# Two neighbouring blocks of convolution sums in one PSUM bank, and the gate stage buffers in pools of their own beside the dense part's first loads

## The chip, the cores and the metric

One core of a Trainium2 chip. The metric is the device time of one execution in microseconds. The kernel before took 3110.72 us, the median of three runs (3105.67 to 3121.32). The engines are TensorE (PE in the profile; its weight loads are PEld), VectorE (DVE), ScalarE (ACT), GpSimd (POOL) and SyncE (SP); matrix products accumulate in PSUM, eight banks of 128 x 512 float32.

## The reference

One decoder layer over 1024 tokens of 1024 channels. What matters here:

```python
z = rmsnorm(h) @ w_in                      # q, k, v, a, gt
attn = dilated_attention(rope(q), rope(k), v)
glu = a * sigmoid(gt)                      # 512 channels
c = causal_depthwise_conv(glu, conv_w) + conv_b     # 31 taps
h += concat(rmsnorm(attn), rmsnorm(silu(layernorm(c)))) @ w_out

# PEER: 8 heads x 16 experts of 16384 for each token
i1, i2, gate = product_key_top16(rmsnorm(h) @ w_q, sub_keys)
act = gelu(x . expert_u[i1 * 128 + i2]) * gate
h += sum(act * expert_v[i1 * 128 + i2])

h += sigmoid(rmsnorm(h) @ w_g) * (p @ w_p)
out = rmsnorm(h)
```

## The kernel before

Tokens lie in 8 tiles of 128, in four groups of two. Each group goes through the **front**: input projection (`qkv`, in `token_major`), attention, convolution (`convolve`), output projection (`mixed`, `project`), the search for experts (`search`, `combine`). The order of the stages is written out at L876 to L888; the projections of the next group start while the group before is still in its convolution and output stage.

PEER is then done in two ways. Tiles 0, 1, 6, 7 (`FEW`) are **gathered**: POOL fetches one row of `expert_u`, later of `expert_v`, per token by an indirect DMA (`fetch`, L609), VectorE multiplies it (L622) or adds it into `gy` (L638); 1024 such rows of 128 tokens in all, which fill VectorE and POOL beside everything else. Tiles 2 to 5 (`ALL`) are done in a **dense** way: a gate for each of the 16384 experts and 512 tokens is built by `gate_matrix` and written to DRAM (`gate_d`), and `dense` runs over all experts in 128 chunks of 128.

*The convolution.* `lin` is a set of three PSUM banks that nearly every projection uses: `q`, `k`, `v`, `a`, `gt`, `o`, `pq`, `pc`, the comparisons `pd`. In `convolve` the 512 channels are four blocks `c` of 128 channels by 256 tokens. For each, 13 taps are done beside (ScalarE scales a `tap`, POOL adds it into `side`, two buffers, L359 to L363), and 18 taps on VectorE, in place in a bank of `lin`, `cs` (L364 to L369). L371 adds the two into `cc`. A `cs` fills 256 of the 512 columns of its bank. The accumulators of `token_major` take one whole bank for each of the two token tiles.

*The seam.* `gate_matrix` fills, for each tile `j` and block `b` of 32 tokens, a `stage` of 128 x 128 x 32 values (two buffers of 16 KB a partition, pool `gp`) and stores it to `gate_d` with one DMA of 2 MB on SyncE's queue (L700). When the 16 stores are issued, `gp` is closed and `dupool` (`du`) is opened at the same place, the right-hand end of SBUF. `du` holds, for `dense`, the chunks of `uT` and their rounded and rest parts (`u`, `uh`, `ul`, two buffers of 4 KB each), `gt` (three buffers of 4 KB) and `gelu` (two of 2 KB).

*The dense part.* `columns(c)` loads chunk `c` of `uT` on SyncE's queue (L728), ScalarE rounds it (`uh`, L730), VectorE takes the rest (`ul`, L732). 24 matmuls (L754 to L756) sum into `ph`, which has two banks. ScalarE's `gelu` (L758) reads it, VectorE multiplies by the gates `gt` (L762), which are read back from `gate_d` (L741). After four chunks, 96 matmuls (L785 to L787) add the products with `expert_v` into `py`.

The order of instructions on each engine and queue is made by the framework's scheduler ahead of time, from its own costs and from the order in the source; it also places the tiles and sets the waits between engines. Memory of a pool that is closed is given to the next pool, whose tiles then wait for the last users of what they lie over.

Of the kernel before, what the change touches and what calls it, by code (L numbers as in the profile page):

```python
# [10 lines left out]
F32 = mybir.dt.float32  # L11
# [9 lines left out]
P = 128  # L21
# [12 lines left out]
DN = ND * P  # L34
# [11 lines left out]
NK = 128  # L46
# [5 lines left out]
GROUP = 4  # L52
BT = 32
# [48 lines left out]
def tile_layer(ctx, tc, t, consts, out):  # L102
    nc = tc.nc
# [6 lines left out]
    uT_d = t["uT"]  # L110
# [10 lines left out]
    def scope(parent, **kw):  # L121
        s = parent.enter_context(ExitStack())
        return s, s.enter_context(tc.tile_pool(bufs=1, **kw))
# [13 lines left out]
    lin, tps, sps, pps = bank(ps, "lin", 3), bank(ps, "tp", 1), bank(ps, "s", 2), bank(ps, "pt", 1)  # L137
# [199 lines left out]
    def convolve(g, xT):  # L337

        gn = xT.shape[2]
        glus = []  # L340
        for c in range(NCT):
            pg = channel_major(xT, w_ag, NCT + c, f"gt{g}_{c}")
            sg = mpool.tile([P, GN], F32, tag="t2", name=f"sg{g}_{c}", bufs=3)[:, :gn]
            S.activation(sg, pg, AF.Sigmoid)
            pa = channel_major(xT, w_ag, c, f"a{g}_{c}")
            glu = apool.tile([P, TAPS - 1 + GN], F32, tag="glu", name=f"glu{g}_{c}", bufs=NCT - 1)[:, : TAPS - 1 + gn]
            V.tensor_copy(glu[:, 0 : TAPS - 1], last[:, c, :])
            V.tensor_tensor(glu[:, TAPS - 1 :], pa, sg, ALU.mult)
            if g + 1 < NG:
                V.tensor_copy(last[:, c, :], glu[:, gn:])  # L350
            glus.append(glu)
        cT = []
        for c, glu in enumerate(glus):
            tap = lambda k: (glu[:, k : k + gn], cw[:, c, k : k + 1])
            side = apool.tile([P, GN], F32, tag="side", name=f"side{g}_{c}", bufs=2)[:, :gn]
            for k in range(SIDE_TAPS):
                xk, wk = tap(k)
                if k == 0:
                    S.activation(side, xk, AF.Copy, scale=wk)  # L359
                else:  # L360
                    m = apool.tile([P, GN], F32, tag="tap", name=f"tap{g}_{c}_{k}", bufs=3)[:, :gn]
                    S.activation(m, xk, AF.Copy, scale=wk)  # L362
                    G.tensor_tensor(side, side, m, ALU.add)  # L363
            sums = lin(f"cs{g}_{c}")[:, :gn]  # L364
            xk, wk = tap(SIDE_TAPS)
            V.tensor_scalar(sums, xk, wk, cw[:, c, TAPS : TAPS + 1], ALU.mult, ALU.add)
            for k in range(SIDE_TAPS + 1, TAPS):
                xk, wk = tap(k)
                V.scalar_tensor_tensor(sums, xk, wk, sums, ALU.mult, ALU.add)  # L369
            cc = apool.tile([P, GN], F32, tag="cc", name=f"cc{g}_{c}", bufs=4)[:, :gn]  # L370
            V.tensor_tensor(cc, sums, side, ALU.add)  # L371
            cT.append(cc)
        return cT
# [273 lines left out]
            gather_v(i, ex, act, y)  # L647
            yield i, y

    def gate_matrix(gp, j, i1, i2, gate):  # L650

        tr = []
        for what, src in (("i2", i2), ("g", gate)):
            f = flat(src)
            if what != "g":
                f32 = mpool.tile([P, SLOTS], F32, tag="t2", name=f"gl{what}{j}", bufs=3)
                S.copy(f32, f)
                f = f32
            pt = pps(f"pgt{what}{j}")
            nc.tensor.transpose(pt[:, 0:P], f, ident)  # L660
            d = gp.tile([P, P], F32, tag=f"{what}T", name=f"{what}T{j}", bufs=2)
            S.copy(d, pt[:, 0:P])
            tr.append(d)
        i2T, gT = tr
        i2N = gp.tile([P, P], F32, tag="i2N", name=f"i2N{j}", bufs=2)
        S.activation(i2N, i2T, AF.Copy, scale=-1.0)
        four = [P, 4, NK]

        def less_keys(ix, t0, name):

            pd = lin(name).rearrange("p (t k) -> p t k", k=NK)
            nc.tensor.matmul(pd, flat(ix), ident16[:, t0 : t0 + 4].unsqueeze(2).to_broadcast(four), start=True, stop=False)
            nc.tensor.matmul(pd, ones16, minus16.to_broadcast([1, 4, NK]), start=False, stop=True)
            return pd

        for b in range(P // BT):
            stage = gp.tile([P, NK, BT], F32, tag="stage", name=f"stage{j}_{b}", bufs=2)
            for o in range(0, BT, 4):
                t0 = b * BT + o
                oa = gp.tile(four, F32, tag="oa", name=f"oa{j}_{t0}", bufs=2)  # L680
                V.scalar_tensor_tensor(
                    oa, less_keys(i1, t0, f"pd1_{j}_{t0}"), 0.0, gT[:, t0 : t0 + 4].unsqueeze(2).to_broadcast(four),
                    ALU.is_equal, ALU.mult,
                )
                o2 = gp.tile(four, F32, tag="o2", name=f"o2_{j}_{t0}", bufs=3)
                if o % 8 == 0:
                    V.tensor_tensor(
                        o2, i2T[:, t0 : t0 + 4].unsqueeze(2).to_broadcast(four),
                        iota.unsqueeze(1).to_broadcast(four), ALU.is_equal,
                    )  # L690
                else:

                    for e in range(4):
                        S.activation(o2[:, e, :], iota, AF.Abs, bias=i2N[:, t0 + e : t0 + e + 1])
                    S.activation(o2, o2, AF.Relu, bias=1.0, scale=-1.0)
                pg = sps(f"pG{j}_{t0}")
                for e in range(4):
                    nc.tensor.matmul(pg[:, rows(e)], o2[:, e, :], oa[:, e, :], start=True, stop=True)  # L698
                S.copy(stage[:, :, o : o + 4], pg.rearrange("p (t i) -> p i t", i=NK))
            nc.sync.dma_start(gd[j, :, :, b], stage.rearrange("p (q c) t -> p q (c t)", c=GROUP))  # L700
# [13 lines left out]
                S.copy(hi, pt)  # L714
                V.tensor_tensor(lo, pt, hi.bitcast(F32), ALU.subtract)

    def dense(du, dp, dus, dps, h1, xh, xl, read):

        phs, pys = bank(dus, "ph", 2), bank(dps, "py", 2)

# [4 lines left out]
        def columns(c):  # L725

            u = du.tile([P, D], F32, tag="u", name=f"u{c}", bufs=2)
            nc.sync.dma_start(u, uT_d[c])  # L728
            hi = du.tile([P, D], F32R, tag="uh", name=f"uh{c}", bufs=2)
            S.copy(hi, u)  # L730
            lo = du.tile([P, D], F32R, tag="ul", name=f"ul{c}", bufs=2)
            V.tensor_tensor(lo, u, hi.bitcast(F32), ALU.subtract)  # L732
            return hi, lo

        ready = columns(0)
        for c0 in range(0, NK, GROUP):
            gts = []
            nb = DN // BT // 2
            for f in range(2):
                gt = du.tile([P, nb, GROUP, BT], F32, tag="gt", name=f"gt{c0}_{f}", bufs=3)  # L740
                nc.sync.dma_start(  # L741
                    gt.rearrange("p (j b) c t -> p j (b c t)", j=ND // 2),
                    gd[f * ND // 2 : (f + 1) * ND // 2, :, c0 // GROUP].rearrange("j p b c -> p j (b c)"),
                )
                gts.append(gt)
            ah, al, vh, vl = [], [], [], []
            for c in range(c0, c0 + GROUP):
# [4 lines left out]
                for k in range(KD):  # L752
# [1 line left out]
                    nc.tensor.matmul(ph, hi, xh[:, k, :], start=k == 0, stop=False)  # L754
                    nc.tensor.matmul(ph, hi, xl[:, k, :], start=False, stop=False)  # L755
                    nc.tensor.matmul(ph, lo, xh[:, k, :], start=False, stop=k == KD - 1)  # L756
                ge = du.tile([P, DN], F32, tag="gelu", name=f"gelu{c}", bufs=2)
                S.activation(ge, ph, AF.Gelu)  # L758
                ge3 = ge.rearrange("p (b t) -> p b t", t=BT)
                for f in range(2):  # L760
                    g = ge3[:, f * nb : (f + 1) * nb]
# [3 lines left out]
                b = dp.tile([P, DN], F32R, tag="al", name=f"al{c}", bufs=GROUP)  # L765
# [7 lines left out]
                b = dp.tile([P, D], F32R, tag="vl", name=f"vl{c}", bufs=GROUP)  # L773
# [67 lines left out]
    fetched, wide, h1s = {}, {}, {}  # L841
# [47 lines left out]
    xh = hilo.tile([P, KD, DN], F32R, name="xh")  # L889
    xl = hilo.tile([P, KD, DN], F32R, name="xl")  # L890
    gph, gp = scope(ctx, name="gph", side="right")
    h1 = dict(zip(sum(GROUPS, ()), sum((h1s[g] for g in range(NG)), [])))
    h1 = [h1[i] for i in ALL]
    ident16 = gp.tile([P, P], BF16, name="ident16")
# [4 lines left out]
    V.tensor_scalar(minus16[:, 0, :], iota[0:1, :], -1.0, None, ALU.mult)  # L899
    stage_search(NG - 1)  # L900
    for j, i in enumerate(ALL):
        gate_matrix(gp, j, *wide[i])
    stage_combine(NG - 1)
    wide_input(h1, xh, xl)
    gph.close()
    den_in, du = scope(ctx, name="dupool", side="right")
    mix.close()
    mix_ps.close()
    ep = ctx.enter_context(tc.tile_pool(name="epool", bufs=1))
# [7 lines left out]
    def read():  # L917

        den_in_ps.close()
        den_in.close()  # L920
        split.close()
        tail = ctx.enter_context(tc.tile_pool(name="tail", bufs=1, side="right"))
        tail_ps = ctx.enter_context(tc.tile_pool(name="tail_ps", bufs=1, space=PSUM, side="right"))
        for f in range(2):
            for k in range(KD // 2 + 1):
                kept[k, f] = embed_weight(tail, f"wt{k}{f}", k, f)
        tails.extend((tail, bank(tail_ps, "pg", 2)))

    dense(du, dp, dus, dps, h1, xh, xl, read)
    den_ps.close()  # L930
    den.close()
    late_ps = ctx.enter_context(tc.tile_pool(name="late_ps", bufs=1, space=PSUM))
# [64 lines left out]
```

## Time and profile before

| | |
|---|---|
| median of three runs | 3110.72 us (3105.67 to 3121.32) |
| the profiled execution | 3121.36 us, its span 3119.6 us |
| TensorE busy | 2736.8 us (88%) |
| VectorE busy | 2505.5 us (80%) |
| POOL busy | 1504.7 us (48%) |
| ScalarE busy | 1129.3 us (36%) |
| mean granted clock of TensorE | 0.948 |
| moved by DMA | 868.89 MB, mean 279 GB/s |

Busy time says what an engine does, and not what the end waits for. For that there are the chain of waits (the work that ended last, followed back step by step), the list of who waited for whom, and the timeline of one engine, where the time an engine sat idle ahead of an instruction stands in brackets with what ended it. A line of a timeline can stand for several instructions of one form (x12); its duration is then that of the whole run. "L369" is a line of the kernel.

### The profile page before, as it was taken

Reading aid. Unit: us, or ns where it says so; the run is one execution under the profiler, and the core shown is the slowest. Engines: PE = TensorE matmul, PEld = TensorE weight load, DVE = VectorE, ACT = ScalarE, POOL = GpSimd, SP = SyncE. Lnnn points to the kernel's source line nnn. Section 1 sums busy time; section 2 is a strip of 40 time slices with the busy share of each in tenths; the row PEclk is TensorE's granted clock in tenths of the full one; section 3 lists DMA queues with packets and bytes.
Section 4 is the critical chain, followed back from the end, with each engine's and each line's share of the span. In section 5 each row is a group of like instructions: output and inputs, shape, how many; then the busy total and the mean of one; then the engine's idle time right before and its main releaser. Section 6 shows DMA issues by size and latency. Waiting matters only on the chain.

```text
span 3119.6 us, 36029 instructions
## 1 busy us (share of the span) xinstructions
PE 2736.8 (88%) x11711; PEld 2003.7 (64%) x11711; DVE 2505.5 (80%) x5164; ACT 1129.3 (36%) x2083; POOL 1504.7 (48%) x1220
## 2 busy tenths in 40 slices
PE   5689969978995789959999999999999999999986
PEld 2456635753773476647777777877777777777543
DVE  1527877988898799968888888988888888888882
ACT  3532534363245249942322222222223223222342
POOL 0300876464445420135665565665565555655670
PEclk9889978989997899989999999999999999999998
DMA  5244869747853866899999999999998999998991
GB/s 193 68 162 129 300 232 353 268 136 278 314 184 121 309 209 179 241 324 330 349 351 326 321 340 333 366 348 337 345 327 321 343 342 338 347 335 299 348 336 58
DMA packets 305390, 868.89 MB, mean 279 GB/s; under 512 B 26874, under 2 KB 93842, under 8 KB 305202
## 3 DMA queue, kind: packets, MB, share of 16 engines
q0 software_dynamic: 147456, 536.94, 47.4%
q1 hardware_dynamic: 154480, 326.30, 30.3%
q10 hardware_dynamic: 3266, 3.36, 0.3%
q8 instruction: 92, 1.51, 0.2%
q14 instruction: 96, 0.79, 0.1%
HBM read 822.98 MB, written 43.52 MB: 278 GB/s over the span
## 4 chain that ended last, share of the span: by engine, by line
PE 32%; DVE 20%; issue 17%; DMA 14%; POOL 11%; ACT 5%; POOLq 0%; ACTq 0%; DVEq 0%; SPq 0%
POOL v L609 5%; DMA v<-in_expert_v_dram 5%; PE pG L698 4%; DVE gy L638 3%; POOL u L609 3%; POOL side L363 3%; DVE u L622 3%; DMA v<-in_expert_v_dram,ex 3%; DMA u<-in_expert_u_dram,ex 2%; PE plg L819 2%; PE pq L270 2%; PE s L389 2%; PE py L785 2%; DVE cs L369 2%; PE py L787 1%
## 5 line engine op out<-in xcount | busy, mean ns | idle before, releaser
L609 POOL DMA_INDIRECT u<-in_expert_u_dram,ex x512 | 675.5, 1319 | 794.4 <-DVE hk L622 508.8
L609 POOL DMA_INDIRECT v<-in_expert_v_dram,ex x512 | 673.6, 1316 | 533.9 <-DVE gy L638 366.3
L638 DVE SCALAR_TENSOR_TENSOR gy<-v,ga,gy 128x1024 f32<-128x1024 f32 x512 | 657.4, 1284 | 41.2 <-DMA v<-in_expert_v_dram,ex 31.7
L622 DVE CUSTOM_DVE_ANT_0 u<-u,gxn 128x1024 f32<-128x1024 f32 x512 | 616.6, 1231 | 46.3 <-DMA u<-in_expert_u_dram,ex 45.1
L754 PE MATMUL ph<-xh,uh 128*128 128x512 f32 x1024 | 405.5, 396 | 47.6 <-ACT uh L730 44.5
L756 PE MATMUL ph<-xh,ul 128*128 128x512 f32 x1024 | 406.9, 397 | 24.8 <-DVE ul L732 24.4
L772 ACT CAST vh<-v 128x1024 fp32r<-128x1024 f32 x128 | 131.5, 1051 | 770.0 <-PE kept_y L787 502.9
L755 PE MATMUL ph<-xl,uh 128*128 128x512 f32 x1024 | 402.4, 393 | 0.0
L363 POOL TENSOR_TENSOR side<-side,tap 128x256 f32<-128x256 f32 x192 | 155.4, 810 | 214.0 <-ACT tap L362 147.5
L754 PEld LDWEIGHTS ph<-xh,uh 128*128 128x128 f32 x1024 | 194.5, 190 | 94.9 <-ACT uh L730 51.8
L756 PEld LDWEIGHTS ph<-xh,ul 128*128 128x128 f32 x1024 | 194.4, 190 | 80.5 <-DVE ul L732 40.1
L774 DVE TENSOR_TENSOR vl<-v,vh 128x1024 fp32r<-128x1024 f32 x128 | 154.2, 1223 | 112.4 <-ACT vh L772 112.2
L785 PE MATMUL py<-vh,ah 128*128 128x512 f32 x512 | 204.0, 398 | 42.3 <-ACT ah L764 42.3
L270 PE MATMUL pq<-x2T,w_pq 128*128 128x256 f32 x1024 | 230.3, 383 | 2.1 <-DMA w_pq<-in_peer_wq_dram 1.5
L755 PEld LDWEIGHTS ph<-xl,uh 128*128 128x128 f32 x1024 | 194.6, 190 | 40.9
L270 PEld LDWEIGHTS pq<-x2T,w_pq 128*128 128x128 f32 x1024 | 194.2, 192 | 30.1 <-issue 2.7
L785 PE MATMUL kept_y<-vh,ah 128*128 128x512 f32 x512 | 201.1, 393 | 0.0
L787 PE MATMUL kept_y<-vh,al 128*128 128x512 f32 x512 | 201.0, 393 | 0.0
L786 PE MATMUL kept_y<-vl,ah 128*128 128x512 f32 x512 | 201.0, 393 | 0.0
L786 PE MATMUL py<-vl,ah 128*128 128x512 f32 x512 | 199.8, 393 | 0.0
L787 PE MATMUL py<-vh,al 128*128 128x512 f32 x512 | 198.4, 395 | 0.3 <-DVE al L766 0.3
L730 ACT CAST uh<-u 128x1024 fp32r<-128x1024 f32 x128 | 134.1, 1048 | 106.6 <-DMA u<-in_uT_dram 74.9
(266 smaller groups left out, 4693.0 us busy)
## 6 DMA issues: line engine op xcount, KB each, us to landing
u<-in_uT_dram SPq DMA_DIRECT2D x128, 512.0 KB, 6.9
v<-in_expert_v_dram SPq DMA_DIRECT2D x128, 512.0 KB, 6.9
w_pq<-in_peer_wq_dram SPq DMA_DIRECT2D x64, 512.0 KB, 5.9
gate_d<-stage SPq DMA_DIRECT2D x16, 2048.0 KB, 10.7
gt<-gate_d SPq DMA_DIRECT2D x64, 512.0 KB, 10.7
w_o<-in_w_out_dram SPq DMA_DIRECT2D x32, 512.0 KB, 4.9
w_k<-in_w_qkv_dram SPq DMA_DIRECT2D x16, 512.0 KB, 4.6
w_q<-in_w_qkv_dram SPq DMA_DIRECT2D x16, 512.0 KB, 3.5
```

What stands on the lines that cost most here:

```text
L270: nc.tensor.matmul(a, w[:, k, :], xT[:, k, :], start=k == 0, stop=k == KD - 1)
L363: G.tensor_tensor(side, side, m, ALU.add)
L609: d = G.indirect_dma_start(out=e, out_offset=None, in_=table, in_offset=bass.IndirectOffsetOnAxis(ap=index, axis=0))
L622: uses(V.tensor_tensor_reduce(out=e, in0=e, in1=xn, scale=1.0, scalar=0.0, op0=ALU.mult, op1=ALU.add, accum_out=hk[:, k : k + 1]))
L638: uses(V.scalar_tensor_tensor(y, e, act[:, k : k + 1], y, ALU.mult, ALU.add))
L754: nc.tensor.matmul(ph, hi, xh[:, k, :], start=k == 0, stop=False)
L755: nc.tensor.matmul(ph, hi, xl[:, k, :], start=False, stop=False)
L756: nc.tensor.matmul(ph, lo, xh[:, k, :], start=False, stop=k == KD - 1)
L774: V.tensor_tensor(b, v, a.bitcast(F32), ALU.subtract)
L785: nc.tensor.matmul(py, ah[e][:, rows(j)], vh[e][:, half(f)], start=first, stop=False)
L786: nc.tensor.matmul(py, ah[e][:, rows(j)], vl[e][:, half(f)], start=False, stop=False)
L787: nc.tensor.matmul(py, al[e][:, rows(j)], vh[e][:, half(f)], start=False, stop=last_e)
```

## The change

Two edits that do not touch each other. In `convolve`, blocks 0 and 1 share one `lin` bank, blocks 2 and 3 another. At the seam, the two stage buffers become two pools `gs0` and `gs1` beside `gp`, used in turn; `dupool` keeps `u`, `uh` and `ul`, and a new `dupool2` gets `gt` and `gelu`; the loads of chunks 0 and 1 of `uT` are issued from ScalarE's queue.

```diff
@@ convolve
-            sums = lin(f"cs{g}_{c}")[:, :gn]
+            if c % 2 == 0:
+                two = lin(f"cs{g}_{c}").rearrange("p (e t) -> p e t", e=2)
+            sums = two[:, c % 2, :gn]
@@ gate_matrix(gp, gs, j, i1, i2, gate)
-            stage = gp.tile([P, NK, BT], F32, tag="stage", name=f"stage{j}_{b}", bufs=2)
+            stage = gs[b % 2].tile([P, NK, BT], F32, tag="stage", name=f"stage{j}_{b}")
@@ dense(du, du2, ...): columns
-            nc.sync.dma_start(u, uT_d[c])
+            (nc.scalar if c < 2 else nc.sync).dma_start(u, uT_d[c])
@@ dense
-                gt = du.tile([P, nb, GROUP, BT], F32, tag="gt", name=f"gt{c0}_{f}", bufs=3)
+                gt = du2.tile([P, nb, GROUP, BT], F32, tag="gt", name=f"gt{c0}_{f}", bufs=3)
-                ge = du.tile([P, DN], F32, tag="gelu", name=f"gelu{c}", bufs=2)
+                ge = du2.tile([P, DN], F32, tag="gelu", name=f"gelu{c}", bufs=2)
@@ after the front
     gph, gp = scope(ctx, name="gph", side="right")
+    gsh, gs = [], []
+    for e in range(2):
+        s, p = scope(ctx, name=f"gs{e}", side="right")
+        gsh.append(s)
+        gs.append(p)
...
     wide_input(h1, xh, xl)
+    gsh[1].close()
+    gsh[0].close()
     gph.close()
     den_in, du = scope(ctx, name="dupool", side="right")
+    den_in2, du2 = scope(ctx, name="dupool2", side="right")
```

## Rows read from the trace of the kernel before

**Rows 1.** The page, first part: the span, and busy us of each engine.
```profile
span 3119.6 us, 36029 instructions
PE 2736.8 (88%) x11711; PEld 2003.7 (64%) x11711; DVE 2505.5 (80%) x5164; ACT 1129.3 (36%) x2083; POOL 1504.7 (48%) x1220
```
**Rows 2.** Windows by stage, dense part: window, length, busy us, clock, DMA share, GB/s.
```profile
2000.00:2400.00 400.00, 378.59 (x1623) 306.10 (x1623) 346.63 (x459) 104.81 (x135) 238.19 (x174) 0.99 0.93 338
```
**Rows 3.** The chain of waits at the seam: start us, us, what.
```profile
1360.96 23.81 DMA gate_d<-stage
1384.96 3.60 DMA u<-in_uT_dram
...
1388.74 1.05 ACT uh L730
```
**Rows 4.** Timeline of SyncE's queue at the seam: start us, us, issue.
```profile
1334.70 12.96 SPq L700 DMA_DIRECT2D gate_d<-stage  x2
...
1385.35 0.94 SPq L741 DMA_DIRECT2D gt<-gate_d  x2
1386.34 0.47 SPq L728 DMA_DIRECT2D u<-in_uT_dram  x1
```
**Rows 5.** Timeline of TensorE: first matmul of chunk 0, and of chunk 2.
```profile
1389.84 0.80 PE L754 MATMUL ph<-xh,uh 128*128 128x512 f32 x1 [29.53 <-ACT uh L730]
...
1402.94 0.39 PE L754 MATMUL ph<-xh,uh 128*128 128x512 f32 x1
```
**Rows 6.** Who waited for whom, TensorE, 360 to 760 us: total us, times, longest.
```profile
PE k L261 <- DVE cc L371: 19.5, 3, 7.0
```
**Rows 7.** Timeline of TensorE: the `k` projections beside the sums of groups 1 and 2.
```profile
421.86 10.53 PE L261 MATMUL k<-w_k,xT 128*128 128x512 f32 x17 [6.99 <-DVE cc L371]
...
684.05 7.01 PE L261 MATMUL k<-w_k,xT 128*128 128x512 f32 x12 [6.63 <-DVE cc L371]
696.97 11.20 PE L261 MATMUL k<-w_k,xT 128*128 128x512 f32 x20 [5.92 <-DVE cc L371]
```
**Rows 8.** Timeline of VectorE: sums of group 0, then ends of blocks in group 1.
```profile
126.42 13.40 DVE L369 SCALAR_TENSOR_TENSOR cs<-glu,cw,cs 128x256 f32<-128x256 f32 x34
...
407.69 0.42 DVE L371 TENSOR_TENSOR cc<-cs,side 128x256 f32<-128x256 f32 x1
...
421.39 0.42 DVE L371 TENSOR_TENSOR cc<-cs,side 128x256 f32<-128x256 f32 x1
...
429.18 0.42 DVE L371 TENSOR_TENSOR cc<-cs,side 128x256 f32<-128x256 f32 x1 [6.42 <-POOL side L363]
```
**Rows 9.** Timeline of POOL: side sums of blocks 2 and 3, group 1.
```profile
410.06 19.09 POOL L363 TENSOR_TENSOR side<-side,tap 128x256 f32<-128x256 f32 x24 [9.08 <-ACT side L359]
```
**Rows 10.** The page, DMA issues: queue, count, KB each, median us to landing.
```profile
u<-in_uT_dram SPq DMA_DIRECT2D x128, 512.0 KB, 6.9
...
gate_d<-stage SPq DMA_DIRECT2D x16, 2048.0 KB, 10.7
gt<-gate_d SPq DMA_DIRECT2D x64, 512.0 KB, 10.7
```
**Rows 11.** Windows of 5 us at the seam: columns as in rows 2.
```profile
1365.00:1370.00 5.00, 0.00 (x0) 0.00 (x0) 1.30 (x4) 0.00 (x0) 3.81 (x4) 0.50 1.09 376
...
1380.00:1385.00 5.00, 0.00 (x0) 0.00 (x0) 0.00 (x0) 0.00 (x0) 0.00 (x0) 0.50 0.69 272
1385.00:1390.00 5.00, 0.16 (x1) 0.16 (x1) 0.18 (x1) 1.04 (x1) 0.00 (x0) 0.50 0.79 254
```
**Rows 12.** Timeline of VectorE near the end: gathered rows added into `gy`.
```profile
3043.81 6.56 DVE L638 SCALAR_TENSOR_TENSOR gy<-v,ga,gy 128x1024 f32<-128x1024 f32 x5
...
3052.68 1.28 DVE L638 SCALAR_TENSOR_TENSOR gy<-v,ga,gy 128x1024 f32<-128x1024 f32 x1
```
**Rows 13.** The chain of waits near the end: transposes of the last closing block.
```profile
3088.01 3.79 PE pt_ple L809 x16
```
**Rows 14.** Groups by line, 0 to 1400 us: busy us, mean ns of one, idle before.
```profile
L369 DVE SCALAR_TENSOR_TENSOR cs<-glu,cw,cs 128x256 f32<-128x256 f32 x272 | 108.2, 480 | 0.0
```

More of the change, by code (lines that the diff above doesn't have):

```diff
@@ L648, in gather_all, with gate_matrix @@
             yield i, y
-    def gate_matrix(gp, j, i1, i2, gate):
+    def gate_matrix(gp, gs, j, i1, i2, gate):
         tr = []
@@ L715, in wide_input, with dense @@
                 V.tensor_tensor(lo, pt, hi.bitcast(F32), ALU.subtract)
-    def dense(du, dp, dus, dps, h1, xh, xl, read):
+    def dense(du, du2, dp, dus, dps, h1, xh, xl, read):
         phs, pys = bank(dus, "ph", 2), bank(dps, "py", 2)
@@ L901, in tile_layer @@
     for j, i in enumerate(ALL):
-        gate_matrix(gp, j, *wide[i])
+        gate_matrix(gp, gs, j, *wide[i])
     stage_combine(NG - 1)
     wide_input(h1, xh, xl)
+    gsh[1].close()
+    gsh[0].close()
     gph.close()
     den_in, du = scope(ctx, name="dupool", side="right")
+    den_in2, du2 = scope(ctx, name="dupool2", side="right")
     mix.close()
@@ L919, in read @@
         den_in_ps.close()
+        den_in2.close()
         den_in.close()
@@ L927, in read @@
         tails.extend((tail, bank(tail_ps, "pg", 2)))
-    dense(du, dp, dus, dps, h1, xh, xl, read)
+    dense(du, du2, dp, dus, dps, h1, xh, xl, read)
     den_ps.close()
```

## The prediction

> **What bounds the kernel now.** I read the page first: the span and the busy shares say that TensorE is the engine with most work, but at 88% it is not busy everywhere [rows 1]. The windows by stage say where: in a stretch from the middle of the dense part it is busy 378.6 of 400 us, with VectorE at 346.6, so there is little to win there [rows 2]. The holes are in the front (before about 1390 us) and at the seam between front and dense part. So I read the chain of waits at the seam next: the last store of the gate matrix takes 23.81 us, then the first chunk of `uT` 3.60, then its rounding on ScalarE 1.05, and only then the first dense matmul starts [rows 3]. SyncE's own list says the same from the other side: the loads of `gt` and of the second `u` are issued only once that store has landed [rows 3, 4]. TensorE idles 29.53 us there [rows 5]. Third, the list of waits in the front, for what TensorE waited on that this change can touch: 19.5 us in three waits of the `k` projection for `cc`, that is for VectorE to give back a bank of `lin` [rows 6, 7].
>
> **Part A: two blocks of sums in one bank.** Removed: two of four `lin` allocations per group, 8 of 16 in all. Added: nothing; 16 x 18 VectorE steps stay as they are. Before, `cs` holds all three `lin` banks at a time, and the two accumulators of the next group's `k` wait for them: the second one beside group 1's sums for the `cc` at 421.39 (6.99 us), both beside group 2's (6.63 and 5.92) [rows 7, 8]. After, one bank is never taken by `cs`, and a second comes back with the `cc` of block 1, in group 1 at 407.69, 14 us before the bank that `k` got [rows 8]. So all three waits can go: 19.5 us of TensorE at most. What is late next: the `cc` of block 3 waits 6.42 us for the side sums, 24 POOL adds in one run of 19.09 us that start only when the `cc` of block 0 frees a `side` buffer [rows 8, 9]; the output projection needs that `cc`, and the change leaves it alone. VectorE, which turns `k` and `q`, also works through gathered rows there, in a fixed order. Bounds: 0 and 19.5 us. I take half, 10, since `k`, `q`, `v` and the output projection follow each other on TensorE, and give back 4 of it: gathered rows that VectorE did in that time move into the dense part, where it has 13% left [rows 2]. Part A: 6 us.
>
> **Part B: the stage buffers in pools of their own, u0 and u1 on ScalarE's queue.** In a block of 128 x 32 gates nothing changes: two stage buffers still alternate. Three edits with one answer, at no cost: `gs0` and `gs1` for one tag with two buffers, `du2` for `gt` and `gelu`, the extra argument. What moves: the right-hand region. By sizes per partition, `gp` without stage is about 14 KB, `gs0` and `gs1` 16 KB each; `du` (`u`, `uh`, `ul`) is 24 KB and so ends inside `gs0`; `du2` lies over the rest of `gs0` and over `gs1`. The last store (block 3) reads `gs1`, so `u`, `uh` and `ul` no longer wait for it; the store before it, out of `gs0`, was issued some 13 us earlier [rows 4] and, at its median of 10.7 us to landing [rows 10], is done by then. Two DMA issues move from SyncE's queue to ScalarE's. Behind them on ScalarE stands its own next step, the rounding of that same `u`, and the previous one, the last stage copy, feeds the store itself; a waiting issue there holds nothing up. On SyncE's queue the issues of `gt`, `v` and the third `u` come up two issues earlier.
>
> New order at the seam: u0 is issued near 1361, lands after some 6.9 us, the median of these loads [rows 10], is rounded in 1.05 us, and TensorE starts near 1369 instead of 1389.84. It has two banks for `ph`, so it does chunks 0 and 1, which took it from 1389.84 to 1402.94, 13.1 us [rows 5], and then waits again: `gelu` lies on `gs1` and needs the store to land, and after it the multiplication needs `gt`, which reads what that store wrote (issued at 1385.35, 10.7 us to landing, so about 1396 [rows 4, 10]). The upper bound is thus 13.1 us, the two chunks. From below: the store shares the DMA engines with 1 MB of `u` more. These are full from 1361 to 1380 (share 1.09 in 1365 to 1370, 376 GB/s) and have room only after (0.69 and 0.79) [rows 11]; 1 MB at 376 GB/s is 2.8 us, an estimate from that row, by which store and `gt` get later. If then nothing is won, part B costs 2.8 us. The free share after 1380, 5 x 0.31 + 5 x 0.21 = 2.6 us of all engines, says that this room is small; the third `u` and the first `v` still queue on SyncE, possibly behind `gt`, and then chunk 2 starts after about 1386.4 + 2.8 + 6.9 + 1.1 = 1397 instead of 1402.94, a gain of 6. I take 8, nearer to that than to 13.1. TensorE's clock stands at the lower level (0.50 granted, 1.2 GHz) in the idle stretch [rows 11]; its rise falls into chunks 0 and 1 instead, off the path.
>
> The row shows full DMA engines while the store runs [rows 11]. The Trainium skill, "DMA: Bandwidth & Descriptors", Issuing engines are not separate DMA queues, says that transfers started by different engines run on the same 16 DMA engines and interleave, so that a second issuing engine saves only issue time. It speaks against the move to ScalarE's queue as a gain in bandwidth; with bandwidth of its own the 2.8 us of delay would fall away, and part B would be some 10.8 us, by the rule it stays 8.
>
> **Sum.** 6 + 8 = 14 us. The profiled execution took 3121.36 us, its span 3119.6 and 1.8 around it; it is 10.6 us above the median and at the upper edge of the three runs. 3121.36 - 14 = 3107; on the median, 3110.72 - 14 = 3096.7, so 3097, 0.45% faster. Does the end carry it? After the dense part eight closing blocks follow one another; the last starts its transposes at 3088.01, while the last gathered row is added at 3052.68, 35 us before it [rows 12, 13]. So the gather does not hold the end unless it falls back by more than that, and a seam 8 us earlier reaches the end.
>
> **Rivals.**
> *Everything carries.* All 19.5 us of part A and 13 of part B: 3110.72 - 32.5 = 3078. For it: TensorE is what the front waits on at both places, and the closing chain has 35 us of room. Against it: `side` on POOL and the full DMA engines.
> *Hidden anyway.* The dense part runs against its transfers and VectorE, and the `k` waits are covered by the wait for `side`: a gain of 0 to 5, 3108. For it: the DMA share of 0.93 in the dense windows [rows 2].
> *The seam stays.* The new `u` still lies over memory that the last store reads, or its issue is ordered behind other work: part A alone, 3105. The rows can't exclude it, the arithmetic of the sizes speaks against it.
> *Slower: the two chains of a bank can't be interleaved.* VectorE now does blocks 0 and 1 tap by tap in turn: 34 steps in 13.40 us, 0.394 each, though one lasts 0.480 [rows 8, 14]. That works because neighbours don't depend on each other; five adds in a row into one `gy` take 6.56 us, 1.31 each for 1.28 of duration [rows 12], so a dependent step starts some 0.03 after the end of the one before. If two halves of one bank count as one thing for the order of work, block 1 can't start before block 0 is done with, its taps step at 0.51 instead of 0.39, and the worst case is 16 x 17 x 0.117 = 32 us, less where gathered rows or block 2 fill the gaps. With part A gone and part B kept: 3110.72 + 32 - 8 = 3135, half covered 3119; I take 3128. It turns the change into a loss once more than 8 us of the 32 stay open, and into one that a measurement shows from some 24 on. Against it: all accesses to these banks are VectorE's, and the side sums could then start earlier, as block 0 ends sooner.
>
> The steps overlap in these rows. The Trainium skill, "VectorE: DVE Perf Modes", The DRAIN you can't avoid, says that the next step does not start until the pipe has emptied, whether or not steps are chained by waits; it adds that a step that nothing holds starts earlier. By its first half the turn-taking would be worth nothing and this rival's price 0 instead of 32 us; the 0.394 us of a step that lasts 0.480 go with the second half, so the price stays.
>
> **How the numbers follow.** Half a per cent, 15.6 us, is about what a measurement of this kernel can tell from no change. Forecast 3097 (3087 to 3106): 0.38. Everything carries, 3078: 0.21. Hidden, 3108: 0.18. Seam stays, 3105: 0.06. Slower, 3128: 0.17, two thirds of it above 3126. Below 3095: 0.21 and half of the forecast's 0.38, so 0.40. Above 3126: 0.12. Between: 0.48. The range from 3076 to 3126 takes in the forecast, both cases without effect, most of the first rival and the mild half of the last.
>
> **What would show it.** Part A: no wait of `k` for `cc` in the list of waits, and `cs` still about 0.39 us a step. Steps of 0.5 us, or `cc` of block 0 ahead of the first tap of block 1, mean the last rival. Part B: two issues of `u` on ScalarE's queue near 1361, the first `ph` near 1369, chunk 2 between 1390 and 1397 on the old time axis, and a second idle time of TensorE ahead of it with `gelu` as its releaser. The forecast is wrong if the dense part is longer than before by what the seam won, if `u` waits for the store as before, or if the order of work elsewhere in the front has changed for the worse.

## The result and the profile after

The changed kernel is slower: 3154.38 us, the median of four runs (3143.73 to 3167.05), against 3116.02 for the kernel before on the same chip (3105.67 to 3125.44). The ratio is 1.0116, its 95% interval 1.0090 to 1.0142. That is 28 us above the upper end of my range. The profiled execution took 3167.05 us, the longest of the four.

Of the page of the kernel after, the span and the busy us of each engine:

```profile
span 3165.2 us, 35984 instructions
PE 2753.2 (87%) x11711; PEld 2012.9 (64%) x11711; DVE 2520.7 (80%) x5164; ACT 1129.8 (36%) x2084; POOL 1534.7 (48%) x1220
```

Beside [rows 1] the span is 45.6 us longer, and no engine works 45 us more: TensorE 16, VectorE 15, POOL 30. The instructions that wait have changed. In the middle of the dense part nothing has moved (window, length, busy us of PE, PEld, DVE, ACT and POOL, clock, DMA share, GB/s; as [rows 2]):

```profile
2000.00:2400.00 400.00, 377.46 (x1615) 304.34 (x1614) 343.59 (x458) 102.44 (x132) 239.53 (x174) 0.99 0.93 336
```

**The seam won what was forecast.** ScalarE's queue, SyncE's queue and TensorE in the timeline of after (start us, us, instruction, idle time ahead of it and what ended it; lines have moved by 2):

```profile
1415.58 0.82 ACTq L730 DMA_DIRECT2D u<-in_uT_dram  x2
...
1416.11 0.52 SPq L702 DMA_DIRECT2D gate_d<-stage  x1
1424.44 9.44 SPq L730 DMA_DIRECT2D u<-in_uT_dram  x2
1441.35 0.93 SPq L743 DMA_DIRECT2D gt<-gate_d  x2
...
1423.21 0.79 PE L756 MATMUL ph<-xh,uh 128*128 128x512 f32 x1 [7.75 <-ACT uh L732]
...
1445.68 0.80 PE L756 MATMUL ph<-xh,uh 128*128 128x512 f32 x1 [7.72 <-ACT gelu L760]
...
1459.92 0.39 PE L787 MATMUL py<-vh,ah 128*128 128x512 f32 x1
```

The two issues of `u` now stand half a microsecond ahead of the last store instead of 24 us behind it. Counted from the issue of that store, the first `ph` comes after 7.1 us instead of 28.9, chunk 2 after 29.6 instead of 42.0 [rows 4, 5], and its releaser is now `gelu`. The 12.4 us won at chunk 2 are 9.1 at the first `py` (43.8 us after the store; before 52.9, by this line of before):

```profile
1413.83 0.39 PE L785 MATMUL py<-vh,ah 128*128 128x512 f32 x1
```

**The front lost 55 us.** The last store is issued at 1416.11 instead of 1360.96 [rows 4]. VectorE in group 0 and in group 1, to be held against [rows 8]:

```profile
126.29 13.40 DVE L371 SCALAR_TENSOR_TENSOR cs<-glu,cw,cs 128x256 f32<-128x256 f32 x34
...
141.07 4.16 DVE L371 SCALAR_TENSOR_TENSOR cs<-glu,cw,cs 128x256 f32<-128x256 f32 x8
...
394.35 12.62 DVE L371 SCALAR_TENSOR_TENSOR cs<-glu,cw,cs 128x256 f32<-128x256 f32 x32
...
407.30 0.41 DVE L373 TENSOR_TENSOR cc<-cs,side 128x256 f32<-128x256 f32 x1
...
408.10 0.54 DVE L368 TENSOR_SCALAR cs<-glu,cw 128x256 f32<-128x256 f32 x1
...
409.75 0.48 DVE L371 SCALAR_TENSOR_TENSOR cs<-glu,cw,cs 128x256 f32<-128x256 f32 x1
410.15 1.22 DVE L624 CUSTOM_DVE_ANT_0 u<-u,gxn 128x1024 f32<-128x1024 f32 x1
...
411.29 0.48 DVE L371 SCALAR_TENSOR_TENSOR cs<-glu,cw,cs 128x256 f32<-128x256 f32 x1
411.69 1.34 DVE L624 CUSTOM_DVE_ANT_0 u<-u,gxn 128x1024 f32<-128x1024 f32 x1
...
424.71 0.70 DVE L347 COPY glu<-last 128x30 f32<-128x30 f32 x1 [7.13 <-ACT tap L362]
...
445.68 0.75 DVE L373 TENSOR_TENSOR cc<-cs,side 128x256 f32<-128x256 f32 x2
...
471.72 0.42 DVE L373 TENSOR_TENSOR cc<-cs,side 128x256 f32<-128x256 f32 x1
```

Before, two chains took turns without a break, between the `cc` at 407.69 and the one at 421.39:

```profile
408.86 12.62 DVE L369 SCALAR_TENSOR_TENSOR cs<-glu,cw,cs 128x256 f32<-128x256 f32 x32
```

After, the `cc` of block 0 comes first (140.02 in group 0, 407.30 in group 1), and only then does block 1 begin its taps (its first step is the one of L368 at 408.10). The lines carry no block numbers. But the 32 steps in 12.62 us ahead of the `cc` of block 0 are two chains in turn, and the `cc` of the second of them comes only at 445.68, beside that of block 1, as does the bank that `k` waits for; so block 0 takes turns with block 2, which lies in the other bank, and blocks 1 and 3 are left to run alone. In group 0, where no gathered rows are on VectorE yet, the taps of block 1 follow one another at 0.52 us. In group 1 a gathered row stands between nearly every two of them, so that they come 1.5 to 1.7 us apart and more. The stretch from 407.71 to 445.68 holds 17 such taps, 16 gathered rows, an idle time of 7.13 us, and two waits for a row's load of 0.75 and 0.97:

```profile
407.00:446.00 39.00, 21.42 (x16) 0.59 0.49 157
```

(the window's length, VectorE's busy us with these rows, their count, then clock, DMA share and GB/s). Rows and idle times are 30.3 of the 38 us; the other 7.7 are the block's own steps. The idle time stands ahead of a copy into `glu` for the next group, which waits for a `tap` of ScalarE, and the taps behind it in VectorE's list wait with it. The last `cc` of group 1 is 42.5 us later than before (471.72, 429.18), that of group 2 55.3 us (758.22, 702.89). In the list of who waited for whom, 360 to 760 us, TensorE pays for it in the very place where I expected a gain [rows 6]:

```profile
PE k L261 <- DVE cc L373: 44.1, 2, 30.4
```

and the longer of the two waits stands in TensorE's timeline, ended by the `cc` of block 1 at 445.68:

```profile
446.15 6.96 PE L261 MATMUL k<-w_k,xT 128*128 128x512 f32 x12 [30.43 <-DVE cc L373]
```

**The end.** Of the 55.2 us that the front lost, 6.1 are back at the last matmul of the dense part (1546.3 us after the last store instead of 1552.4) and 3.4 more in the closing blocks, which makes 45.6. How much of the seam's 12.4 reaches the end in one profile is not to be read finely: from the last store to the end of the dense part, b_only and b5 below, which are one kernel, differ by 7.9 us. The last gathered row is added at 3068.94, 65 us ahead of the last block's transposes at 3134.01 (before 35 [rows 12, 13]); the gather holds nothing here.

### The profile page after: what moved, and what is told of

Its sections match the earlier page's. It is cut to its first block, busy times and chain, and to the rows that moved or that the text cites. A ratio compares the mean times of both kernels' runs of the same rounds, so it can differ in the third digit from the quotient of the medians.

```text
span 3165.2 us, 35984 instructions
## 1 busy us (share of the span) xinstructions
PE 2753.2 (87%) x11711; PEld 2012.9 (64%) x11711; DVE 2520.7 (80%) x5164; ACT 1129.8 (36%) x2084; POOL 1534.7 (48%) x1220
## 5 line engine op out<-in xcount | busy, mean ns | idle before, releaser
L611 POOL DMA_INDIRECT u<-in_expert_u_dram,ex x512 | 682.6, 1333 | 797.3 <-DVE hk L624 526.5
L624 DVE CUSTOM_DVE_ANT_0 u<-u,gxn 128x1024 f32<-128x1024 f32 x512 | 618.2, 1235 | 43.4 <-DMA u<-in_expert_u_dram,ex 38.2
L363 POOL TENSOR_TENSOR side<-side,tap 128x256 f32<-128x256 f32 x192 | 178.9, 932 | 224.9 <-ACT tap L362 139.9
L734 DVE TENSOR_TENSOR ul<-u,uh 128x1024 fp32r<-128x1024 f32 x128 | 155.9, 1218 | 19.9 <-ACT uh L732 19.8
```

What stands on the lines that cost most here:

```text
L611: d = G.indirect_dma_start(out=e, out_offset=None, in_=table, in_offset=bass.IndirectOffsetOnAxis(ap=index, axis=0))
L624: uses(V.tensor_tensor_reduce(out=e, in0=e, in1=xn, scale=1.0, scalar=0.0, op0=ALU.mult, op1=ALU.add, accum_out=hk[:, k : k + 1]))
```

## The experiments

My theory after the traces: the loss is the order of VectorE's steps, in which a shared bank makes the two chains follow each other; the seam is a gain by itself. Rivals: the bank itself is slower, or is held longer; the loss comes from the seam's memory.

### Each edit alone: b_only, a_only

b_only is the changed kernel with

```diff
-            if c % 2 == 0:
-                two = lin(f"cs{g}_{c}").rearrange("p (e t) -> p e t", e=2)
-            sums = two[:, c % 2, :gn]
+            sums = lin(f"cs{g}_{c}")[:, :gn]
```

and a_only is the kernel before with the reverse.

> The seam's edit alone (stage pools of their own, u0 and u1 on ScalarE's queue); each block of sums keeps a bank of its own. Theory 1, the loss is all in the shared bank and the seam wins: the last gate store is issued at 1361 +- 3 us as before, the first dense matmul comes some 21 us earlier than in the kernel before, chunk 2 some 12 us earlier, and the time is 6 to 12 us below the kernel before, 3104 to 3110. Rival, any edit shifts the order of the whole front: the last gate store moves by more than 10 us, and the time is above 3125.

> The shared bank alone. Theory 1: the last gate store near 1416 as in the changed kernel, the seam as before (29 us of idle TensorE), and the time at the changed kernel's plus the 6 to 12 us of the seam, 3160 to 3166. Rival, the seam's edit takes part in the loss: below 3145.

Measured: b_only 3110.38 us, ratio 0.9962 (0.9934 to 0.9991); a_only 3175.2 us, ratio 1.0166 (1.0104 to 1.0228), both against 3123.8 for the kernel before on the same chip. a_only is slower than I had expected (3160 to 3166), by about as much as the kernel before is slower there than beside the changed kernel. The seam is a gain and the shared bank the whole loss. In a_only the last store is issued at 1414.39 and the `cc` of group 1 stand at 404.61, 442.88 and 468.19, as in the changed kernel; in b_only at 1367.36, with the `cc` at 402.97, 404.23, 417.93 and 425.73, in turns as before. I had expected that store at 1361 within 3 us. The same kernel has it at 1362.36 in b5 below, so a difference of 5 us in this place is within what one kernel does.

### Sharing without the order, the order without sharing: cross_b, order_only

cross_b has both edits, but blocks 0 and 2 share a bank, and 1 and 3. order_only is the kernel before, each block in a bank of its own, with one rule of order and no wait: block 1 begins after the `cc` of block 0, block 3 after that of block 2.

```diff
# cross_b
+            if c < 2:
+                twos[c] = lin(f"cs{g}_{c}").rearrange("p (e t) -> p e t", e=2)
+            sums = twos[c % 2][:, c // 2, :gn]
# order_only
-            V.tensor_scalar(sums, xk, wk, cw[:, c, TAPS : TAPS + 1], ALU.mult, ALU.add)
+            first = V.tensor_scalar(sums, xk, wk, cw[:, c, TAPS : TAPS + 1], ALU.mult, ALU.add)
+            if c % 2 == 1:
+                order_after(first.ins, done)
...
-            V.tensor_tensor(cc, sums, side, ALU.add)
+            done = V.tensor_tensor(cc, sums, side, ALU.add).ins.name
```

> Both edits, but blocks 0 and 2 share a bank, and 1 and 3, so that two blocks that VectorE would do in turn lie in different banks; two banks for the sums as in the changed kernel. Theory 1, it is the order of the two blocks in one bank: taps of 0.39 us in turn as before, the waits of k for cc mostly gone, and the time is that of the seam's edit alone or up to 10 us less, 3094 to 3110. Rival, it is the bank that two blocks fill (a step costs more there, or lin lacks banks for others): 3140 or more.

> The kernel before with four banks as before; only an order is added: the first tap of block 1 comes after the cc of block 0, that of block 3 after the cc of block 2, with no semaphore. Theory 1, the order is what costs: taps stand apart with gathered rows between them as in the changed kernel, the last gate store 40 to 60 us later than before, time 3155 to 3170. Rival, the bank costs and not the order: 3116 +- 8.

Measured: cross_b 3113.84 us, ratio 0.9971 (0.9944 to 0.9998); order_only 3160.15 us, ratio 1.0139 (1.0080 to 1.0199). The order alone, with nothing shared, makes a loss that the intervals do not tell from a_only's; its last store is issued at 1404.44, 43 us later than before, where a_only has 53. Sharing alone, with neighbours in different banks, makes none. VectorE in group 1 of cross_b takes turns again:

```profile
402.42 0.41 DVE L373 TENSOR_TENSOR cc<-cs,side 128x256 f32<-128x256 f32 x1
...
403.68 0.41 DVE L373 TENSOR_TENSOR cc<-cs,side 128x256 f32<-128x256 f32 x1
...
404.85 12.62 DVE L371 SCALAR_TENSOR_TENSOR cs<-glu,cw,cs 128x256 f32<-128x256 f32 x32
417.38 0.41 DVE L373 TENSOR_TENSOR cc<-cs,side 128x256 f32<-128x256 f32 x1
```

and in order_only, where it is blocks 0 and 3 that run alone (blocks 1 and 2 take turns), a gathered row follows nearly each tap of such a block, and some of these rows are waited for. Of block 0:

```profile
413.14 0.48 DVE L371 SCALAR_TENSOR_TENSOR cs<-glu,cw,cs 128x256 f32<-128x256 f32 x1
414.66 1.23 DVE L624 CUSTOM_DVE_ANT_0 u<-u,gxn 128x1024 f32<-128x1024 f32 x1 [1.03 <-DMA u<-in_expert_u_dram,ex]
...
415.81 0.48 DVE L371 SCALAR_TENSOR_TENSOR cs<-glu,cw,cs 128x256 f32<-128x256 f32 x1
```

cross_b also tells what the freed bank is worth. Who waited for whom, 360 to 760 us, in cross_b, in order_only, and in b_only, which frees none:

```profile
PE k L261 <- DVE cc L373: 15.0, 2, 7.6
```
```profile
PE k L261 <- DVE cc L373: 56.1, 2, 32.5
```
```profile
PE k L261 <- DVE cc L371: 18.6, 3, 7.3
```

With one `lin` bank never taken by `cs`, `k` waits 3.6 us less, not 18.6, though I had expected these waits mostly gone: it needs two banks, and with this pairing the shared ones come back only with the `cc` of blocks 2 and 3 (in group 1 at 417.38 and 425.25). The 3.6 are hardly clear of what one kernel does (18.6 in b_only, 16.8 in b5). The last store of cross_b, at 1362.39, comes where b5 has it, and its time is no better than b_only's. Whether the two halves are tied because they lie in one bank or because they are parts of one allocation no run separates.

### What stands between the taps: few_before, few_a

The kernel before, and a_only, with 8 of the 128 gathered rows of each table in each of the four gathered tiles; the other 120, and their part of the output, are left out.

```diff
-        for k in range(SLOTS):
+        for k in range(8):
             e = fetch(u_d, ex[:, k : k + 1], f"u{i}_{k}")
```

(and the same for `expert_v`; `hk` is set to zero first.)

> The kernel before with 8 of the 128 gathered rows of each tile (the other rows of tiles 0, 1, 6, 7 are left out, in expert_u and in expert_v), so that VectorE has nearly no gathered rows to do beside the front. It is the base of the next run: blocks in turn at 0.39 us a tap, last gate store somewhat before 1361.

> The shared bank alone, with the same 8 of 128 gathered rows. Theory 1a, most of the price is that gathered rows stand between the taps of a lone block: without them a lone tap takes 0.52 us, the sums of a group last at most 8 us longer than in the run before, and the last gate store is at most 20 us later than there. Rival, the lone chain itself is the price (or the waits of k for its bank): the last gate store 40 us or more later, as with all rows.

Measured, one execution each: 2930.01 and 2938.34 us. The last store is issued at 1302.70 and at 1311.94. The shared bank thus costs 9 us of front where rows are few, and 53 where they are all there: some 44 of the 53 need the rows, give or take the 5 us by which this place moves in one kernel. The last `cc` of group 1 is 6.8 us later (432.71, 425.94) where it is 42.5 with all rows. VectorE in group 1 of few_a:

```profile
408.47 3.64 DVE L371 SCALAR_TENSOR_TENSOR cs<-glu,cw,cs 128x256 f32<-128x256 f32 x7
415.87 0.27 DVE L347 COPY glu<-last 128x30 f32<-128x30 f32 x1 [3.76 <-ACT tap L362]
416.05 5.20 DVE L371 SCALAR_TENSOR_TENSOR cs<-glu,cw,cs 128x256 f32<-128x256 f32 x10
```

The lone taps stand 0.52 us apart, as the last rival of the prediction assumed (0.51).

### Would a freed bank have paid: sums_s_b, few_sums

sums_s_b is b_only with the sums in the two banks of `s`, one block in each, so that `cs` takes no `lin` bank at all. few_sums is the same placement in the kernel before, with 8 rows as above (the rest left out).

```diff
-            sums = lin(f"cs{g}_{c}")[:, :gn]
+            sums = sps(f"cs{g}_{c}")[:, :gn]
```

> The seam's edit, and the sums of the blocks in the two banks of the attention scores (s), one block to a bank, so that lin has all three banks for k and nothing of the order of the blocks is changed. If the waits of k for cc are worth something by themselves: these waits (18.6 us beside the seam's edit alone) are gone and the time is 5 to 12 us below that of the seam's edit alone, 3098 to 3106. Rival, they are covered by the side sums on POOL and by w_o: waits gone, time within 3 us of the seam's edit alone.

> The kernel before with its convolution's sums in the two banks of s, one block in a bank, and with 8 of the 128 gathered rows of each table in each of the four gathered tiles (the other 120 are left out, so is their part of the output). With all rows and the seam edit this placement brought the last store of the gate matrix 25 us earlier and the end of the dense part 20 us earlier, but the end of the kernel came 17 us later. Theory (the gathered rows hold the end: they move out of the shorter front and finish last): with few rows nothing is left to finish late, and what the front wins reaches the end: last store near 1280 (kernel before with 8 rows: 1302.70) and a span shorter by as much, near 2906 (there: 2928.2). Rival (the placement itself costs something behind the front, in the dense part or the closing blocks): the last store comes earlier, but the span is 2918 or more.

Measured: sums_s_b 3130.58 us, ratio 1.0015 (0.9988 to 1.0043), where I expected a gain or the time of b_only. From 360 to 760 us no `k` waits for `cc` any more (it waits 28.3 us for its input `xT` instead), the last store is issued at 1342.22, 25 us earlier than in b_only (20 earlier than in b5), and the last matmul of the dense part starts 20 us earlier (2883). Then the gain is gone: VectorE and TensorE at the end of sums_s_b,

```profile
3091.79 3.93 DVE L638 SCALAR_TENSOR_TENSOR gy<-v,ga,gy 128x1024 f32<-128x1024 f32 x3 [0.69 <-DMA v<-in_expert_v_dram,ex]
...
3097.91 3.79 PE L809 MATMUL pt_ple<-dg,gy 128*128 128x128 f32 x16 [33.12 <-ACT dg L804]
```

where TensorE idles 33.12 us ahead of the last block's transposes, because the last gathered row is added only at 3095.7. In b_only that was at 3055.6. POOL's fetches by stage (window, length, busy us, count, clock, DMA share, GB/s), b_only and then sums_s_b:

```profile
0.00:1340.00 1340.00, 346.73 (x282) 0.92 0.62 215
1340.00:2860.00 1520.00, 883.93 (x645) 0.98 0.93 340
2860.00:3130.00 270.00, 120.50 (x98) 0.92 0.65 236
```
```profile
0.00:1340.00 1340.00, 309.99 (x253) 0.91 0.60 206
1340.00:2860.00 1520.00, 873.66 (x645) 0.98 0.93 338
2860.00:3130.00 270.00, 152.85 (x128) 0.85 0.80 291
```

29 rows fewer are fetched in the front, the dense part takes the same 645 in both, and 30 more are done at the end. few_sums, one execution, speaks against another reason behind the front. With few rows the last store is issued at 1263.80 instead of 1302.70, 38.9 us earlier, and the span is 2889.5 instead of 2928.2 us, 38.7 shorter (I had expected 22 of each): all of the front's gain reaches the end. Its time is 2891.26 us.

### Memory or queue: pools, pools5, b5, actq

pools and pools5 are one kernel: b_only with the loads of `u0` and `u1` on SyncE's queue, as in the kernel before. b5 is b_only again, beside it. actq is the kernel before with nothing but the other queue.

```diff
# pools, pools5: b_only with
-            (nc.scalar if c < 2 else nc.sync).dma_start(u, uT_d[c])
+            nc.sync.dma_start(u, uT_d[c])
# actq: the kernel before with the reverse
```

> The seam's edit without ScalarE's queue: stage pools of their own, u0 and u1 issued on SyncE's queue as before. If the memory is what held u: first dense matmul within 3 us of that with ScalarE's queue (about 8 us after the last store's issue), since nothing stands ahead of u on SyncE's queue. Rival, the queue matters: u0 is issued behind gt or behind the store's landing, first dense matmul some 29 us after the store's issue as before.

> The seam edit without the move to ScalarE's queue (stage buffers, u and gt in pools of their own; u0 and u1 stay on SyncE's queue; the sums in a bank each, as before), against the same edit with the move. One look at it gave 3102.97 us, with u0 issued 0.4 us ahead of the last store and the first ph 7.1 us after it. Theory (what holds u is memory, not the queue): the move brings nothing, so the ratio to the kernel before lies where the seam edit with the move had it, 0.996, within 0.993 to 0.999. Rival a: issued ahead of the store, u0 and u1 come earlier, the ratio of this kernel is lower by another 3 us or more, 0.995 or less, and its py starts earlier in the profile. Rival b: the single look was a good one, and the ratio is 0.998 to 1.000.

> The seam edit with the move of u0 and u1 to ScalarE's queue, beside the version without the move, on the same chip. Theory (the queue brings nothing): its median lies within 5 us of the version without the move; against the kernel before 0.996, as the first time. Rival: the version without the move is faster by over 5 us, since u0 and u1 are then issued ahead of the last store.

> The kernel before with the one edit that u0 and u1 are issued from ScalarE's queue; stage, u and gt lie in one pool as before. Theory (memory holds u, the queue does not): u0 and u1 are issued only when the last store has landed, some 24 us after it was issued, and the first ph starts some 28 us after the issue of the last store, as in the kernel before (28.9); the time is that of the kernel before. Rival: the queue alone lets u go ahead, first ph under 15 us after the last store.

Measured: pools 3102.97 us in one execution; pools5 3109.49 us, ratio 0.9957 (0.9936 to 0.9978); b5 3108.93 us, ratio 0.9958 (0.9942 to 0.9975); actq 3124.26 us in one execution, beside a median of 3123.9 for the kernel before. SyncE's queue in pools5, then ScalarE's queue and TensorE in actq:

```profile
1367.90 0.34 SPq L728 DMA_DIRECT2D u<-in_uT_dram  x1
1368.33 0.53 SPq L700 DMA_DIRECT2D gate_d<-stage  x1
1368.90 14.07 SPq L728 DMA_DIRECT2D u<-in_uT_dram  x2
```
```profile
1388.01 0.87 ACTq L728 DMA_DIRECT2D u<-in_uT_dram  x2
...
1393.62 0.80 PE L754 MATMUL ph<-xh,uh 128*128 128x512 f32 x1 [30.25 <-ACT uh L730]
```

With the pools, `u` is issued beside the store from either queue; with the queue alone it still comes 24 us behind the store (issued at 1364.02) and TensorE idles 30.25 us. The memory was what held it, and the queue brings nothing to the time: the two intervals nearly coincide. In between it does something. Chunk 2 starts 29.2 and 29.5 us after the last store in b_only and b5, and 32.5 and 33.5 in pools and pools5, where the third `u` is issued 14 us after the store instead of 8 or 9; at the first `py` this lead is gone (46.2 and 43.7; 43.3 and 44.4). The single execution of pools was a fast one of this kernel. b5 and pools5 are 0.42% under the kernel before, some 13 us, and b_only 0.38%; the changed kernel is 1.16% above it.

## Why the prediction was wrong

*The step that failed* is the second sentence of part A, "Added: nothing; 16 x 18 VectorE steps stay as they are". The steps stayed and their order did not, and the new order cost 53 us of front (a_only), where the sum of part A has nothing. I had this as the last rival, with 0.17, and held against it that all accesses to these banks are VectorE's. That is no argument: the scheduler orders steps on one engine too, and a_only, cross_b and order_only show that the loss comes with this order and not with the sharing.

*The rival's price was mis-sized too.* I put it at 16 x 17 x 0.117 = 32 us at worst, "less where gathered rows or block 2 fill the gaps". The step of a lone tap was right (0.52 us for 0.51). The count was not: blocks 0 and 2 still took turns, so 8 of the 16 chains run alone, and the same sum gives 16 us; where little else is on VectorE the price is 9 us of front (few_a). The side sums did not start earlier either, which I had held against this rival: in turn with block 2, block 0 has its `cc` at 407.30, before at 406.43. But gathered rows don't fill the gaps, they stretch them: a gap of 0.12 us gets a row of 1.2 us. With all rows there the front lost 53 us (a_only). What I read as a discount was the price: a step in the chain that TensorE waits for comes behind work that nobody waits for.

*Part A's gain* failed with it. The second bank does come back "with the `cc` of block 1", and ends the wait of `k`; but that `cc` stands at 445.68, and not near 407.69 where I had read it off the trace of before. The two things that I took together exclude each other here: neighbours in one bank give it back early only if they take turns, and in one bank they don't; the other pairing, which keeps the turns (cross_b), holds both banks to the end and saves 3.6 us of 18.6. Where the waits do go, in sums_s_b, the front wins 20 to 25 us, all of the 19.5 I allowed, and another sentence fails, that gathered rows "move into the dense part, where it has 13% left": the dense part took 645 fetches in either case and the rows went to the end. That is the condition I had named and not applied, that the gather does not hold the end "unless it falls back by more than that", 35 us: in b_only that room is 27 (3054.33 to 3080.99), and from there to sums_s_b the gather fell back by 40.

*Part B* held in each of its steps. On the old time axis (55.15 us less) the first `ph` starts at 1368.1 (forecast 1369), chunk 2 at 1390.5 (1390 to 1397), with a second idle time that `gelu` ends. The delay of the store by 1 MB of `u`, put at 2.8 us, is 0.9: `gt` is issued 25.2 us behind the last store instead of 24.4. The gain, put at 8 between -2.8 and 13.1, is 12.4 us at chunk 2 and 13 us of the time (0.42% of 3123.9 in b5, interval 8 to 18), at the upper bound, where I chose less; only the size was off. The arithmetic of the sizes, which spoke against the rival in which the seam stays, was right.

The Trainium skill, "DMA: Bandwidth & Descriptors", Issuing engines are not separate DMA queues, gave the 8 us rather than 10.8. Its statement that another issuing engine saves issue time alone agrees with pools5 and b5, whose ratios are 0.9957 and 0.9958. So the 13 us are not bandwidth of a second queue; they come from the earlier issue, which the other memory allows.

*The sum.* The front -55.2, seam and dense part +6.1, closing blocks +3.4: 45.6 us of span. "With part A gone and part B kept" was the right case, with 32 us where 55 belonged.

## What to carry to other kernels

Before two chains of dependent steps are put into one bank, ask whether the order of work still lets them take turns; if a pair must share, share between chains that don't run side by side (blocks 0 and 2 of the kernel before). Where an engine also has long steps that nobody waits for, price a serialized chain not by its own gaps but by the long steps that will stand in them. And a shorter front is worth nothing if the background work that it used to cover then ends last: look at where that work finishes before the gain is counted.

## What the runs showed of the hardware

POOL and VectorE slow each other. POOL's side sums in group 1 of the changed kernel, to be held against [rows 9], where one takes 0.80 us in a run of 24:

```profile
410.95 7.61 POOL L363 TENSOR_TENSOR side<-side,tap 128x256 f32<-128x256 f32 x6 [9.10 <-ACT side L359]
419.68 0.73 POOL L363 TENSOR_TENSOR side<-side,tap 128x256 f32<-128x256 f32 x1
421.54 0.73 POOL L363 TENSOR_TENSOR side<-side,tap 128x256 f32<-128x256 f32 x1
...
427.94 1.79 POOL L363 TENSOR_TENSOR side<-side,tap 128x256 f32<-128x256 f32 x1
```

While VectorE idles (417.6 to 424.7) an add takes 0.73 us; the run of six beside gathered rows takes 1.27 for each, with the short breaks between them, and one add 1.79. The rows feel it too: in the first 1400 us of the changed kernel, the 34 gathered rows of L624 that meet an add take 1.46 us in the mean, the 140 that meet none 1.22. Over the whole kernel the 192 adds take 932 ns each instead of 810. The Trainium skill, "GPSIMD Engine Reference", Specifications, says that GpSimd shares its SBUF interfaces with VectorE, and contends with VectorE instructions that have two SBUF inputs. The gathered row (`u` times `gxn`) has two, and the trace agrees; no run here separates this cause from others. How much of the 44 us that need the rows comes by this way, through a later `side`, stays open.
